# Attention scores of opposite sign, and the keys' copies moved between VectorE and ScalarE, in a one-core encoder layer

## The chip, the core and the metric

The kernel runs on one core of a Trainium2 chip. A core has five engines, each with an instruction queue of its own that it takes in order: TensorE (PE; its weight loads are shown as PEld), VectorE (DVE), ScalarE (ACT), GpSimd (POOL) and SyncE (SP), which here only issues DMAs. They wait for each other through semaphores. The metric is the device time of one execution in microseconds (us); lower is better.

## The reference, cut to what matters

One layer of an encoder over 512 tokens of width 1024, in float32: a layer norm; a mixer with two branches (16 heads of neighbourhood attention, and a bidirectional state space model), merged by sigmoid gates and projected; a layer norm; an MLP with squared ReLU; a layer norm. The change lies in the attention:

```python
def row_block(args):
    r, q_row = args                      # q is scaled by dh ** -0.5 = 0.125
    r0 = jnp.clip(r - kr // 2, 0, rows - kr)
    ...
    bias = rpb[:, dr[None, :, None], dc[:, None, :]].astype(jnp.float32)
    sc = jnp.einsum('bwhd,brwkhd->bhwrk', q_row, k_nb).astype(jnp.float32) + bias[None]
    p = jax.nn.softmax(sc.reshape(bsz, h, GRID_W, kr * kc), axis=-1)
    p = p.reshape(sc.shape).astype(v.dtype)
    return jnp.einsum('bhwrk,brwkhd->bwhd', p, v_nb)
```

The tokens form a grid of 8 rows by 64 columns. Each sees all 8 rows and 16 neighbouring columns, with a bias by relative position.

## The kernel before, in words

**Arithmetic.** TensorE multiplies in a rounded float32 format. To keep accuracy, nearly each operand is split into a high part (the rounded value) and a low part (what is left), and a product is the sum of three: high by high, low by high, high by low (lines 329 to 331, a helper of all projections). The split of a weight slab is made by ScalarE (high, line 311) and VectorE (low, line 312), in two halves each.

**Stages.** First the layer norm, the state space branch and part of the gates, in an order written out by hand (the list `ORDER`). Then the values of the attention are projected. Then comes the attention stage, lines 1252 to 1442, which is the one changed. Then the merge, the output projection, the norm and the MLP. After the hand-written part, the order of each engine's queue is made at build time by the framework's scheduler, which simulates a time line of the program with a cost model; the kernel only adds a few edges. The attention stage is ordered in this way.

**The attention stage.** A loop runs over eight pairs of heads. For a pair:

- The q and k columns of the input weights are loaded and split (`wqk`). TensorE projects q (24 matmuls of 512 columns into `psq`, line 1283), and later k (24 into `psk`, line 1297). Both take turns in two banks of PSUM.
- ScalarE copies `psq` into `qf` with the scale 0.125 (line 1286), then makes the high part in another order of tokens (line 1293); GpSimd makes the low part (line 1295). In `qs`, the high part of a head lies in its own 64 partitions and the low part in the other 64.
- ScalarE copies `psk` into `kf` (line 1300). VectorE rounds each head's half of `kf` twice into `kh`: into the head's own 64 partitions (line 1303) and into the other 64 (line 1304), so that one matmul over 128 partitions gives high by high plus low by high. GpSimd makes the low part of the keys, `klz` (line 1305), whose other half is zero.

For each head of the pair:

- The biases are loaded from DRAM into `raw` (two DMAs of SyncE, one per half of the partitions, line 1316; two buffers), and GpSimd adds the mask for the columns out of reach, two additions of 128x128 into `bias` (line 1321; one buffer).
- TensorE computes the scores of four blocks of 128 queries, two matmuls of 256 columns each (lines 1335 and 1336).
- VectorE adds the bias to a block and takes the row's maximum in the same instruction (line 1347). For block 0, two instructions of 64 partitions do this and read `raw` itself, as no mask is needed there; blocks 1 to 3 take one instruction each, with `bias`.
- VectorE negates the four maxima (line 1350). ScalarE takes the exponentials with them as the bias, with their sums as a second output (line 1352). VectorE inverts the sums (line 1354) and scales the rows (line 1356).
- TensorE transposes the seven blocks of 128 columns (line 1364). ScalarE rounds them (line 1367) and VectorE takes the low part (line 1368). TensorE multiplies by the values (line 1376), and ScalarE and VectorE add the two halves of the result into `aT` (lines 1387 and 1388).

Gate projections (`ps_g`) and the attention's own output projection (`ps_abr`) come in towards the end of the stage.

The constants (an identity, the masks, two triangles) are one DRAM array whose columns are named by `CC_ID` and so on; the mask's columns come into `cst` early in the kernel, by one DMA (line 569).

Of the kernel before, what the change touches and what calls it, by code (L numbers as in the profile page):

```python
# [9 lines left out]
F32 = mybir.dt.float32  # L10
# [3 lines left out]
ALU = mybir.AluOpType  # L14
# [3 lines left out]
P = 128  # L18
# [33 lines left out]

CC_ID = 0
CC_MI = 128
CC_TF = 384
CC_TB = 512
CC_N = 640

# [222 lines left out]
def encoder_layer(ctx, tc, x, w_in, w_attn_br, w_ssd_br, w_o, w_ff1, w_ff2, pcols, rows64,  # L283
# [987 lines left out]
    for t in padded:  # L1271
        nc.gpsimd.memset(t[:, 512:].bitcast(F32), 0.0)

    def by_row(t):
        return t.rearrange("p (r j) -> p r j", r=8)

    def high(k):
        return nc.scalar.activation(aTh[:, k], aT[:, k], AF.Copy)
# [1 line left out]
    for pr in range(NH // 2):  # L1280
        wqk = weights([(w_in, 0, OFF_Q + pr * P, P), (w_in, 0, OFF_K + pr * P, P)], KD, 256, f"qk{pr}")
        psq = psx.tile([P, S], F32, tag="mm", bufs=BANKS["mm"], name=f"ps_q{pr}")
        project(psq, wqk, 0)

        qf = atp.tile([P, S], F32, tag="qf", name=f"qf{pr}")
        nc.scalar.activation(qf, psq, AF.Copy, scale=0.125)
        qs = atp.tile([P, 2, S], F32R, tag="qs", name=f"qs{pr}")
        halves = (slice(0, HD), slice(HD, P))
        for hh, hp in enumerate(halves):
            src = octets(qf[hp])  # L1290
            qh, ql = (in_order(qs[e, hh]) for e in (hp, halves[1 - hh]))
            for sv, hv in ends_first(src, qh):
                nc.scalar.activation(hv, sv, AF.Copy)
            for (sv, hv), (_, lv) in zip(ends_first(src, qh), ends_first(src, ql)):
                nc.gpsimd.tensor_tensor(out=lv, in0=sv, in1=hv.bitcast(F32), op=ALU.subtract)
        psk = psx.tile([P, S], F32, tag="mm", bufs=BANKS["mm"], name=f"ps_k{pr}")
        project(psk, wqk, P)

        kf = atp.tile([P, S], F32, tag="kf", name=f"kf{pr}")
        nc.scalar.activation(kf, psk, AF.Copy)  # L1300
        kh = atp.tile([P, 2, S], F32R, tag="kh", name=f"kh{pr}")
        for hh, hp in enumerate(halves):
            nc.vector.tensor_copy(kh[hp, hh], kf[hp])
            nc.vector.tensor_copy(kh[halves[1 - hh], hh], kf[hp])
            nc.gpsimd.tensor_tensor(out=klz[hp, hh], in0=kf[hp], in1=kh[hp, hh].bitcast(F32),
                                    op=ALU.subtract)
        for hh in range(2):
            h = 2 * pr + hh
            hp = halves[hh]
            kh_g, kl_g = (t[:, hh].rearrange("p (r b j) -> p b r j", r=8, b=4) for t in (kh, klz))  # L1310


            raw = atp.tile([P, 8, 32], F32, tag="raw", bufs=2, name=f"raw{h}")
            base = rpb_pad[h]
            for i, e in enumerate(halves):
                nc.sync.dma_start(
                    raw[e], bass.AP(base.tensor, base.offset + 8 * (1 - i),
                                    [[RPB_W, HD], [8 * RPB_W, 8], [1, 32]]))
            bias = atp.tile([P, 2, 8, 16], F32, tag="bias", name=f"bias{h}")
            for half in range(2):  # L1320
                nc.gpsimd.tensor_tensor(
                    out=bias[:, half], in0=raw[:, :, half * 16 : half * 16 + 16],
                    in1=cst[:, CC_MI + half * P : CC_MI + (half + 1) * P].rearrange(
                        "p (r j) -> p r j", r=8), op=ALU.add)
            sc = atp.tile([P, 7 * P], F32, tag="sc", bufs=2, name=f"sc{h}")
            rows_ = [sc[:, :P]] + [sc[:, m * 256 - P : m * 256 + P] for m in range(1, 4)]
            mx = atp.tile([P, 4], F32, tag="mx", bufs=2, name=f"mx{h}")
            sums = atp.tile([P, 4], F32, tag="sums", bufs=2, name=f"sums{h}")
            for m2 in range(2):
                pss = psx.tile([P, 2, 256], F32, tag="so", bufs=BANKS["so"], name=f"pss{h}_{m2}")  # L1330
                for j in range(2):
                    m = 2 * m2 + j
                    bsl = slice(m - 1, m + 1) if m else slice(0, 4, 3)
                    q = qs[:, hh, m * P : (m + 1) * P]
                    nc.tensor.matmul(pss[:, j, :], q, kh_g[:, bsl], start=True, stop=False)
                    nc.tensor.matmul(pss[:, j, :], q, kl_g[:, bsl], start=False, stop=True)
                for j in range(2):
                    m = 2 * m2 + j
                    if m:
                        runs = [(rows_[m], pss[:, j, :], bias.rearrange("p a r j -> p (a r j)"),  # L1340
                                 mx[:, m : m + 1])]
                    else:
                        runs = [(by_row(rows_[0][e]), by_row(pss[e, 0, (1 - i) * P : (2 - i) * P]),
                                 raw[e, :, i * 16 : i * 16 + 16], mx[e, :1])
                                for i, e in enumerate(halves)]
                    for out_, in0, in1, top in runs:
                        nc.vector.tensor_tensor_reduce(out=out_, in0=in0, in1=in1, scale=1.0,
                                                       scalar=-3.0e38, op0=ALU.add, op1=ALU.max,
                                                       accum_out=top)
            nc.vector.tensor_scalar(out=mx, in0=mx, scalar1=-1.0, scalar2=None, op0=ALU.mult)  # L1350
            for m in range(4):
                nc.scalar.activation(rows_[m], rows_[m], AF.Exp, bias=mx[:, m : m + 1],
                                     accum_out=sums[:, m : m + 1])
            nc.vector.reciprocal(sums, sums)
            for m in range(4):
                nc.vector.tensor_scalar(out=rows_[m], in0=rows_[m], scalar1=sums[:, m : m + 1],
                                        scalar2=None, op0=ALU.mult)

            pts = []
            for n, blocks in enumerate(((6, 0, 1), (2, 3, 4, 5))):  # L1360
                w = len(blocks) * P
                tp = psx.tile([P, w], F32, tag="tr", bufs=BANKS["tr"], name=f"tp_p{h}_{n}")
                for i, b in enumerate(blocks):
                    nc.tensor.transpose(tp[:, i * P : (i + 1) * P], sc[:, b * P : (b + 1) * P], ident)
                pth = padded[h % 2] if n else atp.tile([P, w], F32R, tag="pth", bufs=2, name=f"pth{h}")
                ptl = atp.tile([P, w], F32R, tag=f"ptl{n}", bufs=2, name=f"ptl{h}_{n}")
                high_t = nc.scalar.activation(pth[:, :w], tp, AF.Copy)
                spread = nc.vector.tensor_tensor(out=ptl, in0=tp, in1=pth[:, :w].bitcast(F32),
                                                 op=ALU.subtract)
                pts.append((pth, ptl))  # L1370
            po = psx.tile([P, S], F32, tag="yd", bufs=BANKS["yd"], name=f"po{h}")

            def pv(b, n, at_, ncol, q0, pad=0):
                v = vhl[pr // 4][:, b, pr % 4, 2 * hh : 2 * hh + 2, :]
                for t, width in zip(pts[n], (ncol + pad, ncol)):
                    ins = nc.tensor.matmul(po[:, q0 : q0 + width], v, t[:, at_ : at_ + width],
                                           start=b == 0 and width == ncol and t is pts[n][0],
                                           stop=b == 3 and t is pts[n][1])
                return ins

            pv(0, 0, 192, 192, 0)
            pv(2, 1, 256, 256, 192, 64)
            pv(1, 1, 0, 256, 64)
            last = pv(3, 0, 0, 192, 320)

            low = atp.tile([P, S], F32, tag="low", name=f"low{h}")
            nc.scalar.activation(low[hp], po[HD - hh * HD : P - hh * HD], AF.Copy)
            nc.vector.tensor_tensor(out=octets(aT[hp, pr, :]), in0=in_order(po[hp]),
                                    in1=in_order(low[hp]), op=ALU.add)

        if pr == 3:
            aTh = vpp.tile([P, KD, S], F32R, tag="vhl0", name="aTh")
        elif pr > 3:
            for k in (2 * (pr - 4), 2 * (pr - 4) + 1):
                ins = high(k)
# [413 lines left out]
def constants():  # L1809
# [7 lines left out]
    for half in range(2):  # L1817
        j = half * 16 + i % 16
        d = j[None, :] - qi[:, None]
        ok = (d >= 0) & (d <= 15)  # L1820
        c[:, CC_MI + half * P : CC_MI + (half + 1) * P] = np.where(ok, 0.0, -1e30)
    lm = np.broadcast_to((i[None, :] < i[:, None])[:, None, :], (P, HPG, P)).astype(np.int32)
    return c, np.ascontiguousarray(lm)

# [41 lines left out]
```

## Time and profile before

| what | us |
|---|---|
| time, median of three runs (1180.49 to 1183.59) | 1182.15 |
| the profiled execution's own time | 1182.81 |
| its span, first to last instruction | 1181.0 |
| busy: PE / DVE / ACT / POOL | 1156.1 / 781.0 / 607.1 / 534.2 |
| attention stage, 545 to 712: length | 167.0 |
| in it busy: PE / DVE / ACT / POOL | 159.39 / 137.58 / 107.67 / 72.47 |

A row of a time line has the start, the time, the engine, the line, the operation, what it writes and reads, and how many instructions were merged; in brackets the idle time before it and what ended that. A row of a group has line, engine, operation, operands and count, then the busy time in all (us) and the mean of one (ns), then the engine's idle time before them (us) and its releasers. A row of the waits has who waited for whom, the total in us, how often, and the longest. A busy row of PE is as long as the matmul takes through the array; the next starts before it ends, so that the spacing of the starts is what TensorE needs for one.

### The profile page before, as it was taken

How to read it: one execution, taken by the hardware profiler on the slowest of the kernel's cores; microseconds unless marked ns; L12 is line 12 of the kernel's file. 1: busy time of each engine (PE TensorE's matmuls, PEld its weight loads, DVE VectorE, ACT ScalarE, POOL GpSimd, SP SyncE). 2: the span in 40 equal slices, each digit the busy share in tenths (PEclk: the TensorE clock that was granted, in tenths of full speed). 3: DMA queues.
4: the chain of work that ended last, by engine and by line, in shares of the span. 5: the costliest groups of instructions: out<-in, count | busy, mean ns of one | idle time of the engine just before them, and what ended most of it. 6: DMA issues, size and time to landing. Idle time of an engine off the chain costs nothing.

```text
span 1181.0 us, 16712 instructions
## 1 busy us (share of the span) xinstructions
PE 1156.1 (98%) x6372; PEld 973.4 (82%) x6372; DVE 781.0 (66%) x1355; ACT 607.1 (51%) x994; POOL 534.2 (45%) x522
## 2 busy tenths in 40 slices
PE   8999999999999999999999999999999999999997
PEld 8977888879888888878877888888988888878886
DVE  7758475666567566498888873556543657488856
ACT  6666572846355463555666753342253555365420
POOL 1177967687888776624544411016046131222000
PEclk9999999999999999999999999999999999999999
DMA  6253333343242332476333223444236987888521
GB/s 214 72 187 105 107 108 125 102 125 125 90 149 90 125 131 72 120 147 161 77 89 85 51 72 107 172 144 141 80 107 186 242 194 196 185 210 219 149 78 54
DMA packets 130048, 153.27 MB, mean 130 GB/s; under 512 B 21552, under 2 KB 100528, under 8 KB 129968
## 3 DMA queue, kind: packets, MB, share of 16 engines
q1 hardware_dynamic: 114160, 112.49, 30.3%
q0 software_dynamic: 15232, 38.80, 14.3%
q8 instruction: 50, 0.82, 0.3%
q10 hardware_dynamic: 576, 0.92, 0.2%
q14 instruction: 30, 0.25, 0.1%
HBM read 149.96 MB, written 2.23 MB: 129 GB/s over the span
## 4 chain that ended last, share of the span: by engine, by line
PE 75%; DVE 14%; DMA 4%; ACT 3%; issue 3%; SPq 1%; POOL 0%; DVEq 0%; POOLq 0%; ACTq 0%
PE ps_f L329 8%; PE ps_f L331 8%; PE ps_f L330 8%; PE ps_x L329 5%; PE ps_x L331 4%; PE ps_x L330 4%; PE ps_abr L1425 4%; PE ps_sbr L329 2%; PE ps_sbr L331 2%; PE ps_sbr L330 2%; PE ps_z L329 2%; PE ps_z L331 2%; PE ps_z L330 2%; DMA w2r<-in_w_ff 2%; PE ps_g L330 2%
## 5 line engine op out<-in xcount | busy, mean ns | idle before, releaser
L714 DVE SCALAR_TENSOR_TENSOR cv<-ps_x,pc,cv 128x511 f32<-128x511 f32 (+1 forms) x128 | 95.5, 747 | 31.7 <-ACT cv L706 28.8
L330 PE MATMUL ps_f<-h1Th,wl_f 128*128 128x512 f32 (+1 forms) x288 | 104.1, 365 | 0.0
L329 PE MATMUL ps_f<-h1Th,wh_f 128*128 128x512 f32 (+1 forms) x288 | 103.7, 366 | 0.0
L331 PE MATMUL ps_f<-h1Tl,wh_f 128*128 128x512 f32 (+1 forms) x288 | 102.0, 365 | 0.0
L1628 DVE TENSOR_TENSOR wl_f<-w2r,wh_f 128x1024 fp32r<-128x1024 f32 x42 | 50.0, 1221 | 65.5 <-ACT wh_f L1627 64.9
L329 PE MATMUL ps_z<-wh_z,hTh 128*128 128x256 f32 x256 | 75.9, 297 | 1.0 <-DVE cv L714 1.0
L331 PE MATMUL ps_z<-wl_z,hTh 128*128 128x256 f32 x256 | 71.5, 279 | 0.0
L330 PE MATMUL ps_z<-wh_z,hTl 128*128 128x256 f32 x256 | 71.4, 279 | 0.0
L1622 POOL DMA_DIRECT2D w2r<-in_w_ff x30 | 36.0, 1412 | 75.2 <-DMA w2r<-in_w_ff 48.7
L330 PE MATMUL ps_f<-wh_f,sql 128*128 128x512 f32 x168 | 65.3, 390 | 0.2 <-DVE sql L1628 0.2
L331 PE MATMUL ps_f<-wl_f,sqh 128*128 128x512 f32 x168 | 65.2, 390 | 0.1
L329 PE MATMUL ps_f<-wh_f,sqh 128*128 128x512 f32 x168 | 64.9, 389 | 0.0
L1627 ACT ACTIVATE wh_f<-w2r 128x1024 fp32r<-128x1024 f32 x42 | 42.6, 1052 | 40.8 <-DMA w2r<-in_w_ff 34.0
L329 PEld LDWEIGHTS ps_f<-h1Th,wh_f 128*128 128x128 f32 x288 | 53.9, 188 | 9.2 <-ACT rl L1729 0.3
L330 PEld LDWEIGHTS ps_f<-h1Th,wl_f 128*128 128x128 f32 x288 | 53.9, 188 | 8.7
L312 DVE TENSOR_TENSOR wl_f<-ws_f,wh_f 128x1024 fp32r<-128x1024 f32 x36 | 47.2, 1347 | 20.6 <-ACT wh_f L311 20.1
L331 PEld LDWEIGHTS ps_f<-h1Tl,wh_f 128*128 128x128 f32 x288 | 52.8, 188 | 8.7
L1031 DVE TENSOR_TENSOR ysacc<-ps_sbr,ysacc 128x512 f32<-128x512 f32 x56 | 38.3, 688 | 32.2 <-PE ps_sbr L331 31.8
L329 PE MATMUL ps_x<-hTh,wh_bc 128*128 128x512 f32 (+1 forms) x144 | 57.5, 400 | 0.0
L329 PE MATMUL ps_sbr<-yTh,wh_sbr 128*128 128x512 f32 x128 | 56.7, 443 | 0.1
L329 PE MATMUL ps_x<-hTh,wh_x 128*128 128x512 f32 (+1 forms) x144 | 55.6, 386 | 0.1
L330 PE MATMUL ps_x<-hTh,wl_bc 128*128 128x512 f32 (+1 forms) x144 | 53.2, 369 | 0.4 <-DVE wl_bc L441 0.4
(384 smaller groups left out, 3707.1 us busy)
## 6 DMA issues: line engine op xcount, KB each, us to landing
ws_f<-in_w_ff SPq DMA_DIRECT2D x20, 1024.0 KB, 6.9
w2r<-in_w_ff POOLq DMA_DIRECT2D x18, 1024.0 KB, 8.6
bc<-acs_d SPq DMA_DIRECT2D x32, 512.0 KB, 4.2
w2r<-in_w_ff POOLq DMA_DIRECT2D x30, 512.0 KB, 9.6
ws_bc<-in_w_in SPq DMA_DIRECT2D x16, 512.0 KB, 6.0
ws_x<-in_w_in SPq DMA_DIRECT2D x8, 1024.0 KB, 8.1
ws_z<-in_w_in SPq DMA_DIRECT2D x8, 1024.0 KB, 6.5
ws_g<-in_w_in SPq DMA_DIRECT2D x8, 1024.0 KB, 5.1
```

The source lines that it names most:

```text
L312: (eng[i] if isinstance(eng, tuple) else eng).tensor_tensor(out=lo[:, k], in0=st[:, k], in1=hi[:, k].bitcast(F32), op=ALU.subtract)
L329: nc.tensor.matmul(o, lh, rh, start=start, stop=False)
L330: nc.tensor.matmul(o, ll, rh, start=False, stop=False)
L331: return nc.tensor.matmul(o, lh, rl, start=False, stop=stop)
L714: op("DVE", 0.75, lambda j=j, o=o, n=n: nc.vector.scalar_tensor_tensor(out=acc()[:, o], in0=ps()[:, n], scalar=tap(j), in1=acc()[:, o], op ...
L1031: op("DVE", 0.69, lambda d=d, ps=ps: nc.vector.tensor_tensor(out=ysacc[:, d, :], in0=ps(), in1=ysacc[:, d, :], op=ALU.add), r=[(ps.name, 0 ...
L1425: ins.append(nc.tensor.matmul(pss[j], u, v, start=k + p == 0, stop=k == KD - 1 and p == 2))
L1622: nc.gpsimd.dma_start(t, rows(i, n, c, k), accum_op=ALU.add)
L1627: nc.scalar.activation(hi[:, k], x, AF.Copy)
L1628: low = nc.vector.tensor_tensor(out=lo[:, k], in0=x, in1=hi[:, k].bitcast(F32), op=ALU.subtract)
```

## The change

The sign of everything up to the exponential is turned over. q is scaled by -0.125, the biases are subtracted from a mask of +1e30 in place of being added to one of -1e30, the reductions take minima, and the exponential takes its input times -1 plus the minimum. The negation is left out.

The first copy of the keys (own partitions) is made by VectorE from `psk` in PSUM; the second (other partitions) by ScalarE from `kf`.

The biases get a third part of 128 columns, for block 0. They are made in one operation of GpSimd on 384 columns. `raw` has 48 columns per row for 32, is filled by four DMAs for two, and has one buffer for two. The constants grow by 256 columns. The mask now has 128 columns of zeros (for block 0), then the old two halves; the DMA that fills `cst` has 512 columns for 256.

```diff
-CC_TF = 384
-CC_TB = 512
-CC_N = 640
+CC_TF = 640
+CC_TB = 768
+CC_N = 896
...
-        nc.scalar.activation(qf, psq, AF.Copy, scale=0.125)
+        nc.scalar.activation(qf, psq, AF.Copy, scale=-0.125)
...
         for hh, hp in enumerate(halves):
-            nc.vector.tensor_copy(kh[hp, hh], kf[hp])
-            nc.vector.tensor_copy(kh[halves[1 - hh], hh], kf[hp])
+            nc.vector.tensor_copy(kh[hp, hh], psk[hp])
+            nc.scalar.activation(kh[halves[1 - hh], hh], kf[hp], AF.Copy)
...
-            raw = atp.tile([P, 8, 32], F32, tag="raw", bufs=2, name=f"raw{h}")
+            raw = atp.tile([P, 8, 48], F32, tag="raw", name=f"raw{h}")
             base = rpb_pad[h]
             for i, e in enumerate(halves):
-                nc.sync.dma_start(
-                    raw[e], bass.AP(base.tensor, base.offset + 8 * (1 - i),
-                                    [[RPB_W, HD], [8 * RPB_W, 8], [1, 32]]))
-            bias = atp.tile([P, 2, 8, 16], F32, tag="bias", name=f"bias{h}")
-            for half in range(2):
-                nc.gpsimd.tensor_tensor(
-                    out=bias[:, half], in0=raw[:, :, half * 16 : half * 16 + 16],
-                    in1=cst[:, CC_MI + half * P : CC_MI + (half + 1) * P].rearrange(
-                        "p (r j) -> p r j", r=8), op=ALU.add)
+                for o, n, at_ in ((8 * (1 - i), 32, 16), (8 * (1 + i), 16, 0)):
+                    nc.sync.dma_start(
+                        raw[e, :, at_ : at_ + n],
+                        bass.AP(base.tensor, base.offset + o, [[RPB_W, HD], [8 * RPB_W, 8], [1, n]]))
+            bias = atp.tile([P, 3 * P], F32, tag="bias", name=f"bias{h}")
+            nc.gpsimd.tensor_tensor(
+                out=by_part(bias), in0=by_part(cst[:, CC_MI : CC_MI + 3 * P]),
+                in1=raw.rearrange("p r (a j) -> p r a j", a=3), op=ALU.subtract)
...
                     if m:
-                        runs = [(rows_[m], pss[:, j, :], bias.rearrange("p a r j -> p (a r j)"),
-                                 mx[:, m : m + 1])]
+                        runs = [(rows_[m], pss[:, j, :], bias[:, P:], mx[:, m : m + 1])]
                     else:
-                        runs = [(by_row(rows_[0][e]), by_row(pss[e, 0, (1 - i) * P : (2 - i) * P]),
-                                 raw[e, :, i * 16 : i * 16 + 16], mx[e, :1])
-                                for i, e in enumerate(halves)]
+                        runs = [(rows_[0][e], pss[e, 0, (1 - i) * P : (2 - i) * P], bias[e, :P],
+                                 mx[e, :1]) for i, e in enumerate(halves)]
                     for out_, in0, in1, top in runs:
                         nc.vector.tensor_tensor_reduce(out=out_, in0=in0, in1=in1, scale=1.0,
-                                                       scalar=-3.0e38, op0=ALU.add, op1=ALU.max,
+                                                       scalar=3.0e38, op0=ALU.add, op1=ALU.min,
                                                        accum_out=top)
-            nc.vector.tensor_scalar(out=mx, in0=mx, scalar1=-1.0, scalar2=None, op0=ALU.mult)
             for m in range(4):
-                nc.scalar.activation(rows_[m], rows_[m], AF.Exp, bias=mx[:, m : m + 1],
+                nc.scalar.activation(rows_[m], rows_[m], AF.Exp, bias=mx[:, m : m + 1], scale=-1.0,
                                      accum_out=sums[:, m : m + 1])
...
-        c[:, CC_MI + half * P : CC_MI + (half + 1) * P] = np.where(ok, 0.0, -1e30)
+        c[:, CC_MI + (half + 1) * P : CC_MI + (half + 2) * P] = np.where(ok, 0.0, 1e30)
```

More of the change, by code (lines that the diff above doesn't have):

```diff
@@ L1272, in encoder_layer, with by_part @@
         nc.gpsimd.memset(t[:, 512:].bitcast(F32), 0.0)
-    def by_row(t):
-        return t.rearrange("p (r j) -> p r j", r=8)
+    def by_part(t):
+        return t.rearrange("p (a r j) -> p r a j", a=3, r=8)
     def high(k):
```

## The prediction

> **What bounds the kernel now.** I read the page first, then the stretches of the attention stage (545 to 712 us), which holds every line the change touches, then the timelines of its engines within one pair of heads, then the waits.
>
> ```profile
> span 1181.0 us, 16712 instructions
> ...
> PE 75%; DVE 14%; DMA 4%; ACT 3%; issue 3%; SPq 1%; POOL 0%; DVEq 0%; POOLq 0%; ACTq 0%
> ```
>
> The chain of work that ended last is TensorE's (PE) nearly everywhere; VectorE's 14% (165 us) is in the main this one stage. So the time that can be won here is TensorE's waiting, and not VectorE's work as such. Busy time by stretches, each of the first five one pair of heads long, and then the whole stage:
>
> ```profile
> 583.10:601.40 18.30, 16.69 (x98) 14.03 (x97) 15.81 (x45) 11.55 (x31) 7.70 (x11) 1.00 0.30 73
> ...
> 656.10:674.10 18.00, 18.00 (x105) 15.41 (x103) 15.51 (x45) 13.35 (x33) 7.75 (x11) 1.00 0.25 70
> sum 91.00, PE 85.05 PEld 70.39 DVE 78.61 ACT 60.19 POOL 38.61; mean PE 17.01 PEld 14.08 DVE 15.72 ACT 12.04 POOL 7.72
> ```
>
> ```profile
> 545.00:712.00 167.00, 159.39 (x855) 133.08 (x854) 137.58 (x365) 107.67 (x260) 72.47 (x85) 1.00 0.30 81
> ```
>
> The columns are length, PE, PE's weight loads, VectorE (DVE), ScalarE (ACT), GpSimd (POOL), clock, DMA. TensorE idles 91.00 - 85.05 = 5.95 us in the five pairs and 167.00 - 159.39 = 7.61 us in the stage. Four of the pairs take 18.1 to 18.3 us and leave PE idle; the fifth ran 105 matmuls with gate projections among them, in 18.00 us, and left it no idle time. VectorE is busy 15.7 of 18.2 us. What it does at the turn of a pair, and what PE does meanwhile:
>
> ```profile
> 600.77 0.57 DVE L1303 CAST kh<-kf 64x512 fp32r<-64x512 f32 x1
> 601.37 0.57 DVE L1304 CAST kh<-kf 64x512 fp32r<-64x512 f32 x1
> 601.97 0.57 DVE L1303 CAST kh<-kf 64x512 fp32r<-64x512 f32 x1
> 602.57 1.41 DVE L1304 CAST kh<-kf 64x512 fp32r<-64x512 f32 x1
> 604.01 1.15 DVE L1350 TENSOR_SCALAR mx<-mx 128x4 f32<-128x4 f32 x1
> 605.07 2.35 DVE L312 TENSOR_TENSOR wl_qk<-ws_qk,wh_qk 128x1024 fp32r<-128x1024 f32 x2
> 607.34 0.17 DVE L1354 RECIPROCAL sums<-sums 128x4 f32<-128x4 f32 x1
> ```
>
> ```profile
> 605.19 0.40 ACT L1352 ACTIVATE sc<-sc,mx 128x128 f32<-128x128 f32 x1 [3.39 <-DVE mx L1350]
> ```
>
> ```profile
> 604.24 0.28 PE L1336 MATMUL pss<-klz,qs 128*128 128x256 f32 x1
> 604.36 0.28 PE L1335 MATMUL pss<-kh,qs 128*128 128x256 f32 x1
> ...
> 607.24 0.39 PE L329 MATMUL ps_k<-hTh,wh_qk 128*128 128x512 f32 x1
> 607.47 0.39 PE L330 MATMUL ps_k<-hTh,wl_qk 128*128 128x512 f32 x1
> 609.23 0.52 PE L1364 MATMUL tp_p<-cst,sc 128*128 128x128 f32 x3 [1.37 <-DVE sc L1356]
> ```
>
> The scores of the odd head are done before 600.8, but their negated maxima wait behind four casts for the next pair until 604.01 and for GpSimd until 605.16; only then may ScalarE, idle for 3.39 us, take the exponentials. Reciprocal, scaling and transposes follow, and PE, out of projections after 607.9, stands until 609.23. This is the wait that ends last in the stage.
>
> **What PE needs by itself.** Its rows start 0.23 us apart for 512 columns and 0.12 for 256. A pair has 48 projections and 46 others (16 scores, 14 transposes, 16 value products; those not shown are taken at the scores' spacing, an estimate): 48 x 0.23 + 46 x 0.12 = 16.5 us. Five pairs are 82.5, and the 11 matmuls that the fifth stretch ran beyond 94 are 2.5: 85.0 of the measured 91.0. So 6.0 us can be had there before PE itself is the bound. Outside them the stage idles 7.61 - 5.95 = 1.66 us.
>
> **The change part by part.** Groups and single prices of the stage:
>
> ```profile
> L1304 DVE CAST kh<-kf 64x512 fp32r<-64x512 f32 x16 | 14.8, 927 | 0.5
> ...
> L1303 DVE CAST kh<-kf 64x512 fp32r<-64x512 f32 x16 | 9.6, 599 | 1.9 <-ACT kf L1300 1.7
> L1387 ACT ACTIVATE low<-po 64x512 f32<-64x512 f32 x16 | 9.5, 593 | 4.2 <-PE po L1376 3.9
> ...
> L1350 DVE TENSOR_SCALAR mx<-mx 128x4 f32<-128x4 f32 x16 | 5.2, 323 | 0.4
> ```
>
> ```profile
> L1304 DVE CAST kh<-kf x16: 421/578/1409, 551.5 to 675.3; 64x512 fp32r<-64x512 f32 x16
> ```
>
> ```profile
> L672 DVE COPY acsT<-ps_acsT 32x512 f32<-32x512 f32 x2 | 1.3, 674 | 0.7 <-PE ps_acsT L669 0.7
> ```
>
> *Second copies to ScalarE:* VectorE loses 16 casts, 14.8 us. ScalarE gains 16 copies of 64x512; the trace has that shape from PSUM at 0.593 us, none from SBUF to another half; I take 0.6 (0.5 to 0.7), 9.5 us, 1.2 per pair on an engine busy 12.0 of 18.2. They stand right behind the copy `kf` in ScalarE's queue; queued behind them are the splits of the next weights and the exponentials, and the scores on PE wait for them.
>
> *First copies from PSUM:* the nearest row is a copy of 512 columns from PSUM, 0.674 against 0.599 now (and 0.42 undisturbed): 16 x 0.075 = 1.2 us more, at worst 16 x 0.25 = 4.0. They no longer wait for `kf` but for PE. Behind them on VectorE stand the weight splits. The bank of `ps_k` is held until they have read it; its next user comes a whole query projection later (24 x 0.23 = 5.5 us), so that costs nothing.
>
> *No negation:* 16 x 0.323 = 5.2 us off VectorE, and a hop off the path from scores to exponentials. Each exponential can also start at its own minimum; the trace does not show how early.
>
> VectorE's sum: 14.8 + 5.2 - 1.2 = 18.8 us, 2.35 per pair, and the casts move out from in front of the exponentials. Below, this meets what GpSimd does:
>
> ```profile
> 602.22 2.91 POOL L1305 TENSOR_TENSOR klz<-kf,kh 64x512 fp32r<-64x512 f32 x2
> 612.34 0.88 POOL L1321 TENSOR_TENSOR bias<-raw,cst 128x128 f32<-128x128 f32 x2 [7.22 <-issue]
> ...
> 619.39 1.19 POOL L1321 TENSOR_TENSOR bias<-raw,cst 128x128 f32<-128x128 f32 x2
> ```
>
> ```profile
> 640.61 3.34 DVE L312 TENSOR_TENSOR wl_qk<-ws_qk,wh_qk 128x1024 fp32r<-128x1024 f32 x2
> ```
>
> The cast of 1.41 us and the negation of 1.15 lie exactly under the two `klz` operations, 602.22 to 605.13; a cast has 0.42 at its shortest, and the negation 0.32 on average: they wait for GpSimd. Two pairs later the negation was early, and the weight split in its place took 3.34 instead of 2.35. So part of the 18.8 us is waiting that can move to the splits.
> The Trainium skill has this as a rule (SBUF — State Buffer, Who interferes with whom): a copy or a two-input operation of VectorE with its data in SBUF and a GpSimd instruction shut each other out for a whole instruction, while an operation with at most one SBUF input outside the two-port modes does not take part. By that rule the casts from PSUM are free of GpSimd and the splits of weights are not; the rows above agree as far as they go, and by it alone the sum would be that of the second rival.
>
> *Bias in one operation, minima for maxima, scales of -1:* GpSimd adds 128x384 in one for 128x128 twice (0.88 us together); I take 1.0 (0.9 to 1.8), covered by its idle 7.22 us; without that cover 0.1 us per head, 1.6 in all. The reductions keep their number and columns, so I take no change. The larger constants are 128 KB more at the start, behind the loads that the first matmuls need; I take nothing (0 to 1.6 us, the time of 131 KB at the 81 GB/s of the stage's row).
>
> *Raw biases:* four loads per head for two, and one buffer for two:
>
> ```profile
> L1316 SPq DMA_DIRECT2D raw<-in_rpb_pad x32: 595/634/1540, 539.7 to 672.4; - x32
> ...
> DMA to landing us min/median/max: 2.3/2.5/4.8
> ```
>
> The next head's loads may start when GpSimd has read this head's. Three issues of 0.634 and one landing of 2.5 are 4.4 us, and the addition 1.0: 5.4 us from one addition to the next. The shortest spacing is 612.34 to 619.39, 7.05 us, so 1.6 us are spare and I cost it at nothing. Behind the addition on GpSimd stands `klz`, for which the scores wait; all scores now need the addition, where the first block read `raw` itself.
>
> **Sum.** VectorE gives up more per pair (up to 2.35 us, and the order) than the 1.2 us (6.0 / 5) by which PE waits; PE then bounds. The gain is 6.0 us in the five pairs and nearly all of the 1.66 outside, 1.5: 7.5 us. Span 1181.0 - 7.5 = 1173.5. The profiled execution lasted 1182.81 us, 1.81 above its span and 0.66 above the median of 1182.15; so 1174.7 us. A busy row ends 0.16 us after PE could take the next (0.39 against 0.23, 0.28 against 0.12), so each of some 16 gaps hides as much: 2.6 us more at best; and 1.5 for smaller ones. The stages behind are TensorE's, so the gain lasts to the end.
>
> **Rivals.** *VectorE stays the bound:* the GpSimd waits move whole to the splits. Then the second copies give only 16 x 0.42 = 6.7, the first ones cost 4.0, and the negations give 0 to 5.2: 2.7 to 7.9 us, of which three quarters count: about 4, so 1178. (Three quarters, because the fifth stretch left PE no idle time to win.) For it speaks the row of 3.34; against it, that the exponentials no longer stand behind the casts.
>
> *No change:* ScalarE's second copies come behind other work. Right behind `kf` it now has two halves of a weight split:
>
> ```profile
> 618.03 2.01 ACT L311 ACTIVATE wh_qk<-ws_qk 128x1024 fp32r<-128x1024 f32 x2
> ```
>
> Were the copies queued after those, the keys would be ready 2.0 + 1.2 = 3.2 us after `kf`, and PE would wait for them as it now waits for the transposes. Also PE's queue is written at build time by a scheduler, and its gaps may only move. 1182.
>
> *Slower:* the single raw buffer. SyncE's queue holds the loads of weights too, and these wait:
>
> ```profile
> SPq L303 <- DVE sums L1354: 35.1, 5, 7.1
> ```
>
> That is 7.0 us each time. A bias load behind such a wait comes 7.0 - 1.6 = 5.4 us late; addition and `klz` follow late, and PE has eight projections of 0.23 us to run meanwhile, 1.8 us: 3.6 us lost. Two such pairs eat the gain, and from the third on it decides: three are 10.8 - 7.5 = 3.3 us over, 1185.5; five 1192.7. Against it: now the loads come well before their use, and they would be queued in the order in which the scheduler sees them come free.
>
> **How the numbers follow.** PE bounds (1174.7): 0.52. VectorE stays (1178): 0.20. No change: 0.17. Slower: 0.11. A measurement of this kernel can tell about 0.3% (3.5 us) from no change; the first two lie beyond it: faster 0.72, same 0.17, slower 0.11. The forecast's own range is 7.5 - 2 to 7.5 + 2.6 + 1.5 = 11.6 us of gain; at the low end I allow 12.6 for the last 1.0 of a shorter tail, 1169.5. At the high end no change plus 1.6 of uncovered additions is 1183.8.
>
> **What would show it.** Right: no L1350 row; casts from `ps_k` of 0.6 to 0.7 us that do not stretch under `klz`; exponentials starting within 0.5 us of the last score; pairs of 16.5 to 17 us with PE's idle time under 3 us in the stage; the stage some 7 us shorter and all behind it equal. Wrong: pairs still of 18 us; PE waiting for `kh` from ScalarE; GpSimd's additions waiting for the raw loads; weight splits of 3 us and more in each pair.

## The result and the profile after

The changed kernel takes 1172.66 us (median of 6 runs, 1170.3 to 1174.76), the kernel before 1181.32 us beside it (6 runs). The ratio is 0.9923 [0.9906, 0.9939]: 8.7 us less. The profiled execution lasted 1172.39 us with a span of 1170.6; before it was 1182.81 with 1181.0, so the spans differ by 10.4 us. The profiles show a little more than the medians do, since the profiled execution before was itself 1.5 us above its kernel's median here.

All of it is in the attention stage. Below it reaches from the first copy of a query projection to the last gated output, which takes in the short tail with the gate projections; the columns are those of the prediction's windows (length, PE, its weight loads, VectorE, ScalarE, GpSimd, granted clock, DMA share, GB/s). First the kernel before: the stage, what precedes it, what follows.

```profile
545.50:748.60 203.10, 195.49 (x1014) 162.97 (x1014) 149.96 (x379) 118.46 (x275) 74.39 (x85) 1.00 0.32 88
0.00:545.50 545.50, 536.75 (x3363) 455.86 (x3364) 359.60 (x596) 308.25 (x471) 362.43 (x372) 1.00 0.41 124
748.60:1181.00 432.40, 423.83 (x1998) 354.57 (x1996) 271.43 (x381) 180.39 (x250) 97.39 (x66) 0.99 0.56 156
```

The same three stretches of the changed kernel:

```profile
544.70:737.40 192.70, 191.74 (x1014) 163.41 (x1013) 145.28 (x345) 129.39 (x291) 75.29 (x70) 1.00 0.39 98
0.00:544.70 544.70, 535.30 (x3363) 454.29 (x3364) 356.95 (x598) 308.86 (x472) 363.05 (x371) 1.00 0.42 125
737.40:1170.60 433.20, 424.20 (x1998) 354.95 (x1996) 271.50 (x381) 180.62 (x249) 97.43 (x66) 0.99 0.57 156
```

The stage is 203.10 - 192.70 = 10.4 us shorter, the stretch ahead of it 0.8 shorter and the one behind it 0.8 longer. TensorE runs the same 1014 matmuls. Its idle time falls from 203.10 - 195.49 = 7.61 us to 192.70 - 191.74 = 0.96, which is 6.65 us. The other 3.75 us (195.49 - 191.74) is busy time that the same matmuls no longer show, so a part of the waiting had been hidden in "busy". The prediction reckoned 0.16 us hidden behind each visible gap; of 16 gaps 4 are left, which makes 1.9 us by that price (an estimate). Where the rest was hidden is not shown.

The chain of work that ended last turned from VectorE to TensorE. From the first copy of a query projection to the last output of a head (545.5 to 710.1 us before, 544.7 to 702.5 after) it ran on VectorE for 105.8 us, on ScalarE for 25.8 and on TensorE for 13.1 before; after the change it ran on TensorE for 84.1, on VectorE for 36.1 and on ScalarE for 11.2.

The groups of the stage in the changed kernel (busy us, mean ns, then the idle time before them and who ended it):

```profile
L1321 POOL TENSOR_TENSOR bias<-cst,raw 128x384 f32<-128x384 f32 x16 | 18.7, 1169 | 34.7 <-DMA raw<-in_rpb_pad 18.6 <-DVE mx L1344 7.4 <-DVE ptl L1364 5.5
...
L1303 DVE CAST kh<-ps_k 64x512 fp32r<-64x512 f32 x16 | 11.0, 684 | 4.4 <-ACT kf L1300 4.2
L1304 ACT ACTIVATE kh<-kf 64x512 fp32r<-64x512 f32 x16 | 10.1, 630 | 0.9 <-PE pss L1334 0.7
```

The casts from PSUM take 0.684 us each, the second copies on ScalarE 0.630, the one addition of the bias 1.169. There is no row for a negation. The waits before the exponentials and before the reciprocal that follows them (us in total, times, longest), before the change:

```profile
ACT sc L1352 <- DVE mx L1350: 33.5, 12, 5.7
DVE sums L1354 <- ACT sc L1352: 21.3, 10, 4.5
```

and after it, with the new waits for the raw biases:

```profile
POOL bias L1321 <- DMA raw<-in_rpb_pad: 18.6, 4, 5.8
...
ACT sc L1348 <- DVE mx L1344: 10.0, 9, 2.8
...
DVE sums L1350 <- ACT sc L1348: 5.5, 7, 2.2
```

ScalarE's wait for the extreme values falls from 33.5 to 10.0 us and VectorE's wait for the sums of the exponentials from 21.3 to 5.5: the chain from scores to probabilities is shorter. The waits for GpSimd, which the prediction's first rival held would only move, turn up in the scaling of the probabilities (before L1356, after L1352). Before:

```profile
L1356 DVE TENSOR_SCALAR sc<-sc,sums 128x256 f32<-128x256 f32 x48 | 14.0, 346 | 0.0
...
L1356 DVE TENSOR_SCALAR sc<-sc,sums 128x128 f32<-128x128 f32 x16 | 6.0, 373 | 0.5
```

After:

```profile
L1352 DVE TENSOR_SCALAR sc<-sc,sums 128x256 f32<-128x256 f32 x48 | 24.9, 573 | 0.0
...
L1352 DVE TENSOR_SCALAR sc<-sc,sums 128x128 f32<-128x128 f32 x16 | 8.0, 501 | 0.5
```

The same 64 operations take (24.9 + 8.0) - (14.0 + 6.0) = 12.9 us more. In the trace 22 of the 48 wide ones now run beside a GpSimd operation; these take 0.842 us on average and 1.441 at most, the other 26 take 0.345. Before the change none of the 48 ran beside one. So VectorE's busy time in the stage falls by only 149.96 - 145.28 = 4.7 us, and yet the stage is 10.4 us shorter.

### The profile page after: what moved, and what is told of

The parts are those of the page before. It is cut to its first block, busy times and chain, and to the rows that moved or that the text cites. A ratio compares the mean times of both kernels' runs of the same rounds, so it can differ in the third digit from the quotient of the medians.

```text
span 1170.6 us, 16732 instructions
## 1 busy us (share of the span) xinstructions
PE 1151.2 (98%) x6372; PEld 972.6 (83%) x6372; DVE 773.7 (66%) x1323; ACT 618.9 (53%) x1010; POOL 535.8 (46%) x506
## 4 chain that ended last, share of the span: by engine, by line
PE 77%; DMA 7%; DVE 7%; POOL 3%; ACT 3%; issue 2%; SPq 1%; DVEq 0%; POOLq 0%; ACTq 0%
PE ps_f L329 7%; PE ps_f L331 7%; PE ps_f L330 7%; PE ps_x L329 5%; PE ps_x L331 4%; PE ps_x L330 4%; DMA w2r<-in_w_ff 4%; PE ps_abr L1421 4%; PE ps_z L329 2%; PE ps_sbr L329 2%; PE ps_z L331 2%; PE ps_z L330 2%; PE ps_sbr L331 2%; PE ps_sbr L330 2%; PE ps_g L330 2%
## 5 line engine op out<-in xcount | busy, mean ns | idle before, releaser
L331 PE MATMUL ps_x<-hTl,wh_bc 128*128 128x512 f32 (+1 forms) x144 | 52.9, 367 | 0.7 <-DVE hTl L556 0.7
```

What stands on the lines that cost most here:

```text
L331: return nc.tensor.matmul(o, lh, rl, start=False, stop=stop)
```

## The experiments

The first four kernels ask which part of the change carries the gain. Theory A: the casts no longer stand in VectorE's queue in front of the odd head's exponentials. Theory B: the negation was one hop more between scores and exponentials. Theory C: the build-time scheduler writes another order of the stage, and that order is what counts. Ratios are to the kernel before, run beside each; the change itself stands at 0.9923.

**The keys' copies alone**, the signs, minima, raw biases and negation as before:

```
-            nc.vector.tensor_copy(kh[hp, hh], kf[hp])
-            nc.vector.tensor_copy(kh[halves[1 - hh], hh], kf[hp])
+            nc.vector.tensor_copy(kh[hp, hh], psk[hp])
+            nc.scalar.activation(kh[halves[1 - hh], hh], kf[hp], AF.Copy)
```

> The kernel before with the keys' copies of the change alone: the first ones by VectorE from PSUM, the second ones by ScalarE; signs, negation, biases and buffers as before. Theory A (the casts stood in front of the odd head's exponentials, for their own time and for GpSimd): most of the change's 8.7 us, 5 to 8 us faster than before, and PE's idle time in the attention stage (7.6 us before, 1.0 after) at 3 us or less. Theory B (the negation's hop between scores and exponentials was the wait): 2 us at most. Theory C (the scheduler's new order of PE's queue made the gain, whatever was removed): anything, and no relation between VectorE's busy time and the gain.

1177.24 us, ratio 0.9963 [0.9944, 0.9982]: 4.4 us of gain.

**The signs alone**: the changed kernel with the two lines above put back to the casts of before.

> The changed kernel with the keys' copies put back (both by VectorE from the copy in SBUF): scores of opposite sign, no negation, biases in three parts with one raw buffer. Theory A: 1 to 4 us faster than before, the casts still in front of the exponentials of the odd head. Theory B: 6 us or more. If PE is the bound after either part, the two parts' gains add up to more than 8.7 us; if the parts are independent, to 8.7.

1179.68 us, 0.998 [0.9968, 0.9993]: 2.4 us of gain. Theory A had asked for 5 to 8 us from the copies and 1 to 4 from the signs, theory B for 2 at most and 6 or more: A fits better, and neither part brings the whole by itself; 4.4 + 2.4 = 6.8 us is short of 8.7, though the intervals (2 us to each side) don't exclude a plain sum.

**The raw biases loaded once**, ahead of the loop over heads, from the changed kernel, so that no head waits for a load. All heads then use the biases of the first; the other 15 sets are left out:

```
-            raw = atp.tile([P, 8, 48], F32, tag="raw", name=f"raw{h}")
-            base = rpb_pad[h]
...
+    raw = atp.tile([P, 8, 48], F32, tag="raw", name="raw")
+    base = rpb_pad[0]
```

> The changed kernel with the raw biases loaded once, before the loop over heads, so that every head takes head 0's biases: GpSimd's 18.6 us of waiting for the raw loads, and 60 of 64 loads, are gone. Theory A (PE bounds, the single raw buffer costs nothing): within 1.5 us of the changed kernel. Rival (the single buffer takes part of the gain): 2 to 5 us faster than the changed kernel.

1172.65 us, 0.9924 [0.9901, 0.9946]. The 18.6 us that GpSimd waits for raw biases in the changed kernel cost nothing that can be told (the interval is 2.7 us to each side).

**The hop put back**: the changed kernel with a multiplication of the four minima by 1.0 where the negation stood.

```
+            nc.vector.tensor_scalar(out=mx, in0=mx, scalar1=1.0, scalar2=None, op0=ALU.mult)
             for m in range(4):
                 nc.scalar.activation(rows_[m], rows_[m], AF.Exp, bias=mx[:, m : m + 1], scale=-1.0,
```

> The changed kernel with a VectorE operation on the minima put back where the negation stood (times 1.0 in place of times -1.0): 16 small operations, which also make all four exponentials wait for all four minima again. Theory A: 0 to 2 us slower than the changed kernel, since VectorE and ScalarE have room now. Theory B: 4 us or more slower.

1181.37 us, 0.9999 [0.9986, 1.0012]: with sixteen operations of a third of a microsecond the whole gain is gone. Theory A had allowed 2 us. Their row, and the waits of this kernel:

```profile
L1347 DVE TENSOR_SCALAR mx<-mx 128x4 f32<-128x4 f32 x16 | 5.4, 337 | 0.2
```

```profile
ACT sc L1349 <- DVE mx L1347: 26.5, 13, 3.9
...
DVE sums L1351 <- ACT sc L1349: 20.8, 13, 2.2
```

Both waits are back near the 33.5 and 21.3 us of before. They do not price the loss, though: in the kernel with the keys' copies alone the same two waits are 23.4 and 20.5 us, and it is 4.1 us faster than this one. VectorE in one head, in order of time (start, length):

```profile
614.74 0.42 DVE L1344 CUSTOM_DVE_ANT_0 sc<-pss,bias 128x256 f32<-128x256 f32 x1
615.08 0.08 DVE L1344 DVE_READ_ACCUMULATOR2_ANT mx<- 128x1 f32 x1
615.08 0.69 DVE L1365 TENSOR_TENSOR ptl<-tp_p,pth 128x512 fp32r<-128x512 f32 x1
615.68 1.71 DVE L312 TENSOR_TENSOR wl_qk<-ws_qk,wh_qk 128x1024 fp32r<-128x1024 f32 x1
617.32 0.16 DVE L1347 TENSOR_SCALAR mx<-mx 128x4 f32<-128x4 f32 x1
```

The last minimum is there at 615.16. The operation itself takes 0.16 us, but a subtraction and half of a weight split stand before it in VectorE's queue, and it comes at 617.32. That suggested a sharper form of B: not the operation costs but its place in a full queue. The remaining kernels take the hop apart. It contains the operation (theory O), a join, since all four exponentials wait for the last of four minima (J), and a second visit to VectorE's queue (Q).

**The join alone**: the first three exponentials of a head are made to wait for its last reduction, with no operation in between.

```
+                if m < 3:
+                    behind(e_, top_, "all four minima")
```

> The changed kernel with a wait alone added: the exponentials of blocks 0 to 2 of a head wait for the reduction of block 3, with no operation put in. Theory J (what the negation cost was that it gathered four minima, so that 2.0 us of exponentials stand behind the last score): 5 to 9 us slower than the changed kernel, like the kernel with the operation put back (1181.4). Theory O (the small operation itself, its queueing on VectorE behind GpSimd and its hop): within 2 us of the changed kernel. Theory C (the scheduler's order): not tied to either.

1170.61 us, 0.9921 [0.99, 0.9942]: no cost that can be told, though the order of the matmuls moved with it (see below). VectorE's wait for the exponentials doubles against the changed kernel's 5.5 us, and the time stays:

```profile
DVE sums L1352 <- ACT sc L1348: 11.5, 8, 2.5
```

J falls, unless the moved order made up for its cost. That each exponential can start at its own minimum is worth nothing that can be measured.

**One small operation for each block's own minimum**, so without a join:

```
+                nc.vector.tensor_scalar(out=mx[:, m : m + 1], in0=mx[:, m : m + 1], scalar1=1.0,
+                                        scalar2=None, op0=ALU.mult)
                 nc.scalar.activation(rows_[m], rows_[m], AF.Exp, bias=mx[:, m : m + 1], scale=-1.0,
```

> The changed kernel with a small VectorE operation (times 1.0) on each block's own minimum, 64 in place of 16, so that no exponential waits for another block's. Theory J: at most 4 us slower than the changed kernel, although VectorE has four times the small operations (some 10 us of busy time). Theory O: 9 us or more slower, more than the kernel with 16 operations.

1176.94 us, 0.9966 [0.995, 0.9983]: about half of the gain goes, some 5 us. That lies between the 4 at most of theory J and the 9 or more of theory O.

**The same operation on ScalarE**, in the queue of the exponentials and directly ahead of them:

```
+            nc.scalar.activation(mx, mx, AF.Copy)
```

> The changed kernel with one operation more in each head between the last reduction and the exponentials, a copy of the four minima onto themselves, as in the kernel that brought the whole gain back, but on ScalarE, directly ahead of the exponentials in ScalarE's own queue. Theory Q, the cost of the old negation was its place in VectorE's queue (weight splits, casts and subtractions stand between the last reduction and it): 16 small ScalarE operations of some 0.2 us, 3 us of ScalarE's time, and no further visit to VectorE, so 1172 to 1175.5 us. Rival C, any further step in this chain makes the scheduler write another and worse order of the stage: 1178 to 1182 us, as with the operation on VectorE.

1178.9 us, 0.9987 [0.9969, 1.0004]. Here Q fails: without any second visit to VectorE most of the gain goes all the same, to where theory C had put it (1178 to 1182). Its row and the waits:

```profile
L1347 ACT ACTIVATE mx<-mx 128x4 f32<-128x4 f32 x16 | 3.3, 205 | 17.1 <-DVE mx L1344 16.9
```

```profile
DVE sums L1351 <- ACT sc L1349: 16.1, 8, 3.6
```

**The operation on VectorE, its result unread**: it goes to a tile of its own, and the exponentials don't wait.

```
+            mc = atp.tile([P, 4], F32, tag="mc", bufs=2, name=f"mc{h}")
+            nc.vector.tensor_scalar(out=mc, in0=mx, scalar1=1.0, scalar2=None, op0=ALU.mult)
```

> The changed kernel with the same small operation per head on VectorE (four minima times 1.0), but into a tile of its own that nothing reads: the exponentials don't wait for it. Theory Q, the wait of the exponentials for a second visit to VectorE's queue is what costs: without it 1172 to 1174.5 us. Rival O, VectorE's time itself counts (16 operations of 0.33 us, 5.3 us): 1176 to 1178 us. Rival C, the further instruction makes another and worse order: 1178 to 1182 us.

1169.83 us, 0.993 [0.9901, 0.9959]: no cost that can be told (3.4 us to each side, from five executions), although the operation was more stretched than where it was read:

```profile
L1348 DVE TENSOR_SCALAR mc<-mx 128x4 f32<-128x4 f32 x16 | 9.4, 585 | 0.3
```

```profile
DVE sums L1352 <- ACT sc L1350: 2.1, 4, 0.8
```

O falls too: it had asked for 1176 to 1178 us, and 9.4 us more on VectorE change nothing. The loss goes with a step on which the exponentials depend, on whichever engine it runs. Of theory C a part is excluded. Count, in the traces, how many of the 1136 matmuls of scores, transposes, values and projections for heads and gates would at least have to move to give the order of the changed kernel: 0 with the raw biases loaded once, 4 with the unread operation, 120 with the join. All three are as quick as the change. With the step on VectorE it is 161, on ScalarE 183, on each block 285; all three lose. But a moved order is not slower as such: the next two kernels move 198 and 302 and lose nothing. Whether the step costs by its own length, or because the scheduler arranges the stage otherwise around it, stays open: in no kernel here does the step stand in an unchanged order.

**The first copies from SBUF** (the first line of the pair reads `kf[hp]` again, the second stays on ScalarE):

> The changed kernel with the keys' first copies from the copy in SBUF again, the second ones still by ScalarE. Theory A (PE bounds after the change; freedom from GpSimd and from the wait for the copy is worth little): within 2 us of the changed kernel, the casts at 0.42 to 1.4 us each with GpSimd in parallel. If the source in PSUM matters by itself: 3 us or more slower.

1173.18 us, 0.9935 [0.9913, 0.9957]: no difference from the change.

**Both copies by VectorE, both from PSUM:**

```
-            nc.scalar.activation(kh[halves[1 - hh], hh], kf[hp], AF.Copy)
+            nc.vector.tensor_copy(kh[halves[1 - hh], hh], psk[hp])
```

> The changed kernel with the second copies back on VectorE, but from PSUM: VectorE gains 16 copies of 0.69 us (11 us), ScalarE loses 16 of 0.63 (10 us). If VectorE has room now (PE bounds): 0 to 3 us slower than the changed kernel. If VectorE's load is what the copies' move was worth: 4 us or more slower.

1172.54 us, 0.9933 [0.9913, 0.9953]: no difference either. Two of its rows:

```profile
L1352 DVE TENSOR_SCALAR sc<-sc,sums 128x256 f32<-128x256 f32 x48 | 14.0, 347 | 0.0
L1304 DVE CAST kh<-ps_k 64x512 fp32r<-64x512 f32 x16 | 11.0, 689 | 0.5
```

VectorE has 11.0 us of casts back, and the scaling is at its old 347 ns; the 10.9 us by which the 48 wide scalings are stretched in the changed kernel (24.9 against 14.0) are gone too. For the time it is all one. ScalarE is not needed for the gain of the copies: in the kernels tried it is enough that VectorE does not make both casts from the copy in SBUF. (It does so where the gain is small, in the kernel with the signs alone.)

**Is PE the bound?** From both kernels one of the three products of the query projection is left out, 64 matmuls of 0.227 us, 14.5 us of PE's work and of no other engine's:

```
-        project(psq, wqk, 0)
+        for k in range(KD):
+            nc.tensor.matmul(psq, wqk[0][:, k, :P], hTh[:, k, :], start=k == 0, stop=False)
+            nc.tensor.matmul(psq, wqk[1][:, k, :P], hTh[:, k, :], start=False, stop=k == KD - 1)
```

> The kernel before, with one of the three products of each part of the query projection left out (the low part of the normalized rows against the high part of the weights): 64 matmuls of 512 columns fewer, 8 in each pair, which PE started 0.227 us apart, so 14.5 us less of PE's work and nothing less for any other engine. Theory P, PE bounds this stage only in part before (7.6 us of it idle, and more idle time in front of matmuls that only look busy): the other engines' chain shows through, and the kernel falls by clearly less than 14.5 us, by 7 to 11 us, with more than 12 us of PE idle in the stage. Rival, the idle time before is a fixed latency that adds to PE's work whatever that is: the kernel falls by the whole 14.5 us, to about 1167, with the idle time at 7 to 8 us.

> The changed kernel with the same 64 matmuls left out. Theory P: PE is the bound of the stage after the change (0.96 us idle), so that it falls by more than the kernel before did under the same cut, by 11 to 14.5 us, to 1158 to 1162; the distance between the two cut kernels is wider than 8.7 us. Rival, PE's idle time was traded for another engine's limit just behind it: the cut brings at most 5 us and PE's idle time in the stage grows by 9 us or more.

The kernel before, thinned in this way, takes 1178.72 us, 0.9992 [0.9975, 1.0009] of the full one: 14.5 us of matmuls less, and nothing gained that can be told. The thinned changed kernel takes 1165.93 us, 0.9865 [0.9839, 0.9892]; against the change's own 0.9923 this is 0.58%, 6.9 us. The stages, before and after, each thinned:

```profile
541.80:744.80 203.00, 186.95 (x954) 157.19 (x953) 155.01 (x380) 117.74 (x275) 81.43 (x85) 0.96 0.32 89
```

```profile
546.60:734.70 188.10, 180.91 (x954) 153.82 (x953) 140.44 (x347) 128.87 (x291) 77.05 (x70) 0.99 0.41 101
```

Before, the stage stays at 203.0 us. It holds 60 matmuls fewer (a part of the first projection lies ahead of it), 13.6 us of PE's work. Of these, 8.4 turn up as idle time (203.00 - 186.95 = 16.05, against 7.61) and 5.1 in matmuls that take longer (186.95, where 195.49 - 13.6 = 181.9 were left). The granted clock accounts for those: it was at half for 17.1 us, of which PE was busy for 13.1, so that an estimated 6.6 us of its work were lost (the last section). After, the stage shrinks by 192.70 - 188.10 = 4.6 us; 6.2 go into idle time (7.19 against 0.96) and 2.8 into slower matmuls (an estimated 1.6 of them by the clock, with 3.2 us busy at half).

So theory P holds in its order and not in its sizes: it forecast 7 to 11 us for the kernel before and 11 to 14.5 for the changed one, and about 1 and 6.9 came. These runs do not separate three things: the other engines' chain, the clock at half, and a new order (of the 944 matmuls of heads and gates without the query projections, 326 stand elsewhere than before, and 255 elsewhere than in the changed kernel). That the other engines' chain set the pace before rests on the chain of the result section and on the 8.4 us of new idle time. The change shortened it until PE stands just ahead of it: with some 5 us less of PE's work, idle time comes back. Thinned, the two stages are 14.9 us apart, and 10.4 when full. These 4.5 us more say nothing of the chain, as the clock alone took 6.6 - 1.6 = 5.0 us more from the kernel before.

## Why the prediction was right, and what was mis-sized

*Direction and size.* 7.5 us less were forecast, 8.7 measured; 1172.66 us lies 2.0 below the forecast 1174.7, inside the forecast's own range. "The stages behind are TensorE's, so the gain lasts to the end" held within 0.8 us. That the number came out so near is in part luck: two steps of the path to it, VectorE's sum and the place of the second copies, did not come about as forecast.

*PE's waiting.* Of the visible idle time 7.5 us were taken and 6.65 went. The mis-sized term of the sum is the hidden waiting, left out of the forecast and allowed as "2.6 us more at best; and 1.5 for smaller ones": it gave 3.75 in the profiled pair, nearly the whole 4.1. Where a gap is visible, the time hidden behind it should have been counted as likely and not as a bound.

*"PE then bounds"* is right by a margin of a few microseconds only: the thinned kernel shows the next limit close behind. The forecast gave VectorE's 18.8 us as more than enough, though it said that a part could move, and that reckoning by VectorE's busy time is where its reasoning failed. VectorE gave up 4.7 us, not 18.8, and 9.4 us added to it cost nothing. Of the signs that it named, PE's idle time under 3 us came (0.96), and so did shorter pairs: from the third copy `kf` to the seventh 16.8 us each, where it was 18.2.

*No negation.* The forecast credited it with "5.2 us off VectorE, and a hop off the path", and priced only the first. It was the other way round: the operation's time is worth nothing, and putting the step back, with the order that comes with it, costs up to 9 us. The change is only 4.7 us faster than the keys' copies alone, which have the step too. Why the hop put back is slower than those, 0.9999 to 0.9963, isn't settled. Their orders differ by 40 of the 1136 matmuls only; but the hop put back also has the single raw buffer and the bias in one addition, and its clock was at half for 6.8 us of the profiled stage, against 3.4. That each exponential starts at its own minimum, which the forecast left unpriced, is worth nothing that can be told.

*The copies.* The prices were right: 0.6 taken and 0.630 found on ScalarE, 0.674 and 0.684 from PSUM. Under `klz` the casts don't stretch any more:

```profile
L1303 DVE CAST kh<-ps_k x16: 651/688/695, 549.4 to 669.1; 64x512 fp32r<-64x512 f32 x16
```

The longest takes 0.695 us, where the casts from SBUF had reached 1.409. On these casts the rule of the Trainium skill that the prediction named (SBUF — State Buffer, Who interferes with whom) agrees with the trace. "The casts move out from in front of the exponentials" came true only by half. In one pair of the changed kernel the two that are left stand, with a weight split ahead of them, between the second and the third block's reduction of the odd head:

```profile
580.14 2.35 DVE L312 TENSOR_TENSOR wl_qk<-ws_qk,wh_qk 128x1024 fp32r<-128x1024 f32 x2
582.41 1.40 DVE L1303 CAST kh<-ps_k 64x512 fp32r<-64x512 f32 x2
583.84 0.42 DVE L1344 CUSTOM_DVE_ANT_0 sc<-pss,bias 128x256 f32<-128x256 f32 x1
```

And two kernels show that neither the PSUM source of the first copies nor ScalarE for the second is needed.

*The rival that VectorE stays the bound* (waits for GpSimd move whole) came true in its mechanism and not in its price. They moved, though to the scaling and not to the weight splits, whose mean stayed; before and after:

```profile
L312 DVE TENSOR_TENSOR wl_qk<-ws_qk,wh_qk 128x1024 fp32r<-128x1024 f32 x13 | 19.3, 1516 | 0.1
```

```profile
L312 DVE TENSOR_TENSOR wl_qk<-ws_qk,wh_qk 128x1024 fp32r<-128x1024 f32 x12 | 17.3, 1472 | 3.3 <-ACT wh_qk L311 3.1
```

Both copies from PSUM take 10.9 of these 12.9 us away again, and the time doesn't move: VectorE's stretched rows are not what the stage waits for.

*The rival of no change* had ScalarE's second copies come behind the two halves of a weight split. So they did, in all eight pairs, and not "right behind the copy `kf`", the step of the forecast that failed here. In five pairs exponentials went ahead of them as well. They start 1.9 to 5.0 us after `kf` ends; in the pair shown above:

```profile
577.05 0.59 ACT L1300 ACTIVATE kf<-ps_k 128x512 f32<-128x512 f32 x1
577.53 2.00 ACT L311 ACTIVATE wh_qk<-ws_qk 128x1024 fp32r<-128x1024 f32 x2
...
580.87 1.27 ACT L1304 ACTIVATE kh<-kf 64x512 fp32r<-64x512 f32 x2
```

The rival's condition came true and its price did not: the profile shows no wait of PE for these copies, and its scores wait 0.4 us in all for VectorE's. In the new order PE has projections of the next pair to run meanwhile, and takes this pair's first scores at 587.71. The forecast had not reckoned with that. The rival's second leg, that the scheduler's order could undo the gain, is the part left open above.

*The slower rival* and the cost of the single raw buffer: 5.4 us were reckoned from one addition to the next and held to fit. The chain of waits of the changed kernel (start, length) shows one case:

```profile
589.26 1.01 POOL bias L1321
590.28 0.61 SPq L1317
590.93 0.64 SPq L1317
591.61 0.64 SPq L1317
592.29 3.65 DMA raw<-in_rpb_pad
...
596.10 1.37 POOL bias L1321
```

From one addition to the next it took 596.10 - 589.26 = 6.8 us, as the load landed in 3.65 and not in 2.5, and GpSimd did wait, 18.6 us in four places, which the forecast had named as a sign of being wrong. "I cost it at nothing" was right all the same: the kernel without any such wait is no quicker.

## What to carry to other kernels

Price a small operation by who depends on it, not by its duration or its engine: 0.2 to 0.34 us on which the exponentials waited went with a loss of 5 to 9 us over 16 heads, 0.585 us that nobody read with none, and a bare join of four results with none either. How much of the loss is the step itself, and how much the order that a scheduler makes around it, these runs leave open. Where PE's row shows idle gaps, take work away from PE alone before you call it the bound; here 14.5 us of matmuls less gave nothing that can be told before the change and about half after it. Read the clock beside it, as a PE that waits can be slowed too. Busy time that an edit takes off VectorE is not a gain until something that ends last waits for it.

## What the runs showed of the hardware

The clock that TensorE is granted falls to half in a stage that stays above 90% busy. In the thinned kernel before, PE stands still for 3.91 us (start, length; in brackets the idle time):

```profile
583.63 0.28 PE L1338 MATMUL pss<-klz,qs 128*128 128x256 f32 x1
587.82 0.53 PE L1378 MATMUL po<-pth,vhl 128*128 128x192 f32 x1 [3.91 <-ACT pth L1369]
```

and in the columns of the windows the clock (third from the end) is at 0.88 in the first row and at 0.50 in the next two, PE being at work again in the last:

```profile
583.80:585.80 2.00, 0.11 (x1) 0.00 (x0) 0.66 (x3) 2.00 (x9) 1.84 (x4) 0.88 0.00 0
585.80:587.80 2.00, 0.00 (x0) 0.00 (x0) 1.94 (x9) 2.00 (x4) 0.93 (x1) 0.50 0.00 0
...
589.80:591.80 2.00, 2.00 (x8) 1.71 (x8) 2.00 (x5) 0.00 (x0) 1.74 (x2) 0.50 0.00 0
```

A mean of 0.88 over these 2 us means that the clock fell at about 585.3, some 1.4 us after PE's last matmul had ended at 583.91. No such long gap is needed. In the kernel with the hop put back, PE was busy for 2.05 of 3.40 us, with no gap above 0.7, and then the clock was at 0.53 on average for 3.6 us:

```profile
621.60:625.00 3.40, 2.05 (x10) 1.29 (x9) 3.31 (x12) 2.71 (x7) 1.99 (x4) 1.00 0.69 244
```

```profile
625.00:628.60 3.60, 3.60 (x10) 2.83 (x9) 1.53 (x5) 2.40 (x9) 3.41 (x3) 0.53 0.02 5
```

```profile
625.39 0.63 PE L330 MATMUL ps_k<-hTh,wl_qk 128*128 128x512 f32 x1
625.82 0.63 PE L331 MATMUL ps_k<-hTl,wh_qk 128*128 128x512 f32 x1
```

The matmuls of 512 columns then start 0.43 us apart in place of 0.23. The Trainium skill (TensorE: Matmul & The Clock Gate, Part 1: The HAM clock gate) says that the clock goes to half after an idle window of about 3.4 us and comes back after a busy one. On the fall the traces differ: in the first case PE had stood still for 1.4 us only, in the second the window was 60% busy (2.05 of 3.40). On the return they agree: in the first case the clock was full again at 592.2, after 3.41 us in which PE was busy for 2.83. In the clock records of the fourteen traces, the falls within one trace lie whole multiples of 3.41 us apart, and in the 3.41 us before each of them PE was busy for 2.06 us at most.

So waiting on PE costs twice, once as idle time and once as slower matmuls behind it. In the stage of the thinned kernel before, PE was busy for 13.1 us at half clock, an estimated loss of 6.6 us.
